# A two-block layer on one core: the second block's stores, and the transfers of its sums, issued from GpSimd's queue instead of SyncE's

## The chip, the core and the metric

The kernel runs on one core of one Trainium2 chip. The metric is the time of one execution on the device in microseconds, as the median of three runs. Engines are named as the profile names them: PE is TensorE (PEld its loading of weights), DVE is VectorE, ACT is ScalarE, POOL is GpSimd, and SP is SyncE, which computes nothing and issues transfers. SPq is SP's queue. A transfer can be issued from SP's queue or from POOL's, and each queue issues in its order: an instruction at its head that waits holds all behind it.

## The reference, cut to what matters

Two layers follow one another on 1,024 tokens of width 1,024, in float32. The first has a gated spatial branch, a state-space branch and 16 experts with 128 tokens each; the change doesn't touch it. The second, the subject here, projects its input to queries, keys, values, gates, a recurrent branch and merge gates, mixes dilated attention of three groups of four heads, runs a linear recurrence over time, and merges:

```python
h = rms_norm_2(x, g_pre) * (1 + scale) + shift
proj = h @ w_in
q, k, v, g_att, u, g_lru, merge = jnp.split(proj, split_at, axis=-1)
y_a = (dilated_attention(q, k, v) * jax.nn.silu(g_att)) @ w_pa
u = causal_depthwise_conv(u, conv_w, conv_b)
y_b = (rg_lru(u, ...) * jax.nn.silu(g_lru)) @ w_pb
gate_a, gate_b = jnp.split(jax.nn.sigmoid(merge), 2, axis=-1)
out = (gate_a * y_a + gate_b * y_b) @ w_o
return x + gate * rms_norm_2(out, g_post)
```

## The kernel before

Float32 products are made of parts: each operand is split into a high part (ScalarE, line 224, `wh`) and the rest (VectorE, line 225, `wl`), and three matmuls of 128x128 by 128x512 replace one (`mm3`).

The second block (`block2`) starts at about 1,700 us. Its projections go in pairs of 128 output columns (`Pair`, numbered by `n`): a scheme of seven products P1 to P7 instead of eight, for the two column blocks and the two halves of the tokens. For that, the pair's weights are loaded into two buffers `wr` (of four; line 217), VectorE forms sums of them (lines 505 to 508), and parts A, B, C, D are split. Pair n+1's weights are asked for when pair n has begun; split D and split C of an earlier pair free the buffers.

What a product leaves in PSUM goes through `one` or `two` of an output object. `Spill` copies or adds it into a tile `st` of 128x512 (two buffers) and stores it to DRAM (lines 416 and 418): queries, keys and values (`qd`, `kd`, `vd`; 24 stores each), the gate of the recurrence (`sgd`, 16), the attention gate (`gad`, 8) and the merge gates (`mgd`, 32). With `step` 8 (queries and keys of group 2) the store writes 1,024 runs of 256 bytes. `Merge` does the same for `yd` (16 stores, lines 440 and 446). `Keep` leaves the recurrent input in SBUF.

Three generators run beside the projections, one step per product (`tick`). `lru` makes the recurrence of one block of 128 channels and stores the result to `hgd` (line 646). `sums` then loads these results in pairs (lines 655 and 656), forms four sums and differences on GpSimd (lines 660 to 667, 128x512 each; four quarters of four) and stores them to `hs1d` to `hs4d` (line 670), for use as operands of the last projections. `attention` works head by head: loads of v, q and k (lines 690, 694, 695), scores, softmax, values, and a store of the head's result with its sums to `od` (lines 758, 761, 763; rows of 520 bytes); then it combines the groups and stores `otd` (line 830). `sums` and `attention` use the same six buffers `m0` to `m5`; the first q and k come into those that held the third quarter of `sums`.

Before the change GpSimd's queue in this block held one scatter, a few splits and subtractions at the start, eight small memsets (line 464) and the sixteen additions of `sums`. Everything that is transferred was issued from SyncE. The order of every queue is made when the kernel is built, by a scheduler that goes by the order of the program and by its own estimates of when an operand or a buffer will be ready. In the experts' part, three loads of weights are issued from GpSimd (line 1918).

Of the kernel before, what the change touches and what calls it, by code (L numbers as in the profile page):

```python
# [364 lines left out]
def block2(k, out, dbg=None):  # L365
    nc, i, c = k.nc, k.i, k.c
    V, S, SY, GP = nc.vector, nc.scalar, nc.sync, nc.gpsimd
# [3 lines left out]
    halves = [slice(0, 512), slice(512, 1024)]  # L371
# [18 lines left out]
    class Spill:  # L390
# [11 lines left out]
        def one(s, h, p):  # L402
            st, (o, p) = s.of(p)
            S.activation(o, p, AF.Copy)
            s.put(h, st)

        def two(s, h, a, b):
            st, (o, a, b) = s.of(a, b)
            V.tensor_tensor(o, a, b, op=ADD)  # L409
            s.put(h, st)  # L410

        def put(s, h, st):
            if s.step == 8:

                d = s.dst.rearrange("p (r h i) -> p h r i", r=8, h=2)
                SY.dma_start(d[:, h], st.rearrange("p (r i) -> p r i", r=8))
            else:
                SY.dma_start(s.dst[:, halves[h]], st)

    class Keep:  # L420
        def __init__(s, dst):
# [8 lines left out]
    class Merge:  # L430
# [6 lines left out]
        def one(s, h, p):  # L437
            st = k.t([128, 512], "st", 2)
            V.tensor_tensor(st, p, s.gate[:, halves[h]], op=MUL)
            SY.dma_start(s.dst[:, halves[h]], st)  # L440

        def two(s, h, a, b):
            st = k.t([128, 512], "st", 2)
            V.tensor_tensor(st, a, b, op=ADD)  # L444
            V.tensor_tensor(st, st, s.gate[:, halves[h]], op=MUL)  # L445
            SY.dma_start(s.dst[:, halves[h]], st)

    hgd = [dram(f"hgd{f}") for f in range(8)]
    hsd = {n: [dram(f"h{n}d{x}") for x in range(2)] for n in ("s1", "s2", "s3", "s4")}
# [42 lines left out]
    class Pair:  # L492
# [9 lines left out]
        def sums(s, eng=V):  # L502
            s.t = k.t([128, 1024], "t12")
            (a0, a1), (b0, b1), (t0, t1) = ((z[:, :512], z[:, 512:]) for z in (*s.raw, s.t))
            eng.tensor_tensor(t0, b0, a0, op=SUB)
            eng.tensor_tensor(t1, b1, t0, op=SUB)
            eng.tensor_tensor(b0, b1, b0, op=SUB)
            eng.tensor_tensor(a1, a1, t1, op=SUB)
# [81 lines left out]
    def lru(f, u):  # L590
        fs = slice(f, f + 1)
        uc, r = k.m(1, 1152), k.m(2, 1152)
        SY.dma_start(uc[:, 1024:], i["wrg"][:, f * 128:(f + 1) * 128])
        SY.dma_start(r[:, 1024:], i["wig"][:, f * 128:(f + 1) * 128])
        ws = [tuple(k.t([128, 128], n + q, 1, FR) for q in "hl") for n in ("wrg", "wig")]
        for raw, w in zip((uc, r), ws):
            k.split(raw[:, 1024:], *w)
        uc, r = uc[:, :1024], r[:, :1024]
        cw = cq("cw")[:, 4 * f:4 * f + 4]
        S.activation(uc, u[:, 3:], AF.Identity, scale=cw[:, 0:1], bias=cq("cb")[:, fs])  # L600
        for j in (1, 2, 3):
            V.scalar_tensor_tensor(uc, u[:, 3 - j:1027 - j], cw[:, j:j + 1], uc, op0=MUL, op1=ADD)
            yield
        if "uc" in dbg:
            SY.dma_start(dbg["uc"][f * 128:(f + 1) * 128, :], uc)
        yield
        uh, ul = k.split(uc, k.m(4, 1024, FR), k.m(3, 1024, FR))
        yield
        P = []
        for wh, wl in ws:  # L610
            for hs in halves:
                P.append(k.ps("pb"))
                k.mm3(P[-1], wh, wl, uh[:, hs], ul[:, hs], True, True)
            if not P[2:]:
                yield
        ig, d = k.m(3), k.m(4)
        for p, (b, o, hs) in zip(P, ((b, o, hs) for b, o in (("brg", r), ("big", ig)) for hs in halves)):
            S.activation(o[:, hs], p, AF.Sigmoid, bias=cq(b)[:, fs])
        yield
        V.tensor_tensor(uc, ig, uc, op=MUL)  # L620
        t = ig
        S.activation(t, r, AF.Tanh, scale=p4[:, fs])
        S.activation(r, r, AF.Exp, scale=m8[:, fs])
        yield

        S.activation(r, r, AF.Copy, scale=0.5, bias=0.5)
        V.scalar_tensor_tensor(d, t, 1.0, r, op0=ADD, op1=MUL)
        yield
        V.scalar_tensor_tensor(r, d, -2.0, r, op0=ADD, op1=MUL)
        S.activation(t, t, AF.Sqrt)  # L630
        yield
        V.tensor_scalar(d, r, -2.0, -1.0, op0=MUL, op1=ADD)
        yield
        V.scalar_tensor_tensor(r, r, -2.0, t, op0=MUL, op1=MUL)
        sg = k.m(3)
        SY.dma_start(sg, sgd[f])
        yield
        S.activation(sg, sg, AF.Silu)
        V.tensor_tensor(uc, uc, r, op=MUL)
        yield  # L640
        V.tensor_tensor_scan(out=r, data0=d, data1=uc, initial=0.0, op0=MUL, op1=ADD)
        if "lru" in dbg:
            SY.dma_start(dbg["lru"][f * 128:(f + 1) * 128, :], r)
        yield
        V.tensor_tensor(r, r, sg, op=MUL)
        SY.dma_start(hgd[f], r)

    def sums():

        lo, hi = halves  # L650
        todo = None
        for x in range(5):
            if x < 4:
                g, r, t = (k.m(3 * (x % 2) + y) for y in range(3))
                SY.dma_start(g, hgd[x])
                SY.dma_start(r, hgd[x + 4])
                yield
            if todo:
                put, g_, r_, t_ = todo
                GP.tensor_tensor(t_[:, lo], g_[:, hi], r_[:, hi], op=ADD)  # L660
                put("s1", t_[:, lo])
                GP.tensor_tensor(g_[:, hi], g_[:, lo], g_[:, hi], op=SUB)
                put("s3", g_[:, hi])
                yield
                GP.tensor_tensor(t_[:, hi], t_[:, lo], g_[:, lo], op=SUB)
                put("s2", t_[:, hi])
                GP.tensor_tensor(r_[:, lo], r_[:, lo], t_[:, hi], op=SUB)
                put("s4", r_[:, lo])
                yield
            todo = (lambda n, z, x=x: SY.dma_start(hsd[n][x // 2][:, halves[x % 2]], z)), g, r, t  # L670


    toks = [[(128 * m, 1) for m in range(8)],
# [7 lines left out]
    otd = [dram(f"otd{j}") for j in range(4)]  # L681
    tok = lambda g, m: slice(toks[g][m][0], toks[g][m][0] + 127 * toks[g][m][1] + 1, toks[g][m][1])

    class Head:
# [53 lines left out]
        def values(s, u):  # L738
            ms, W = tiles[s.g][u]
            g, n = s.g, len(ms)  # L740
            if u == 0:
                s.R = k.m(5, 1040).rearrange("p (m d) -> p m d", m=8)
            p = k.ps("pb")
            vv = lambda m: s.v[:, m * 128:(m + 1) * 128]
            for x, m in enumerate(ms):
                o = p[:, x * 128:(x + 1) * 128]
                if W == 256:
                    k.mm(o, s.pt[:, 2 * x * 128:2 * x * 128 + 128], vv(m - back[g]), True, False)
                    k.mm(o, s.pt[:, 2 * x * 128 + 128:2 * x * 128 + 256], vv(m), False, True)
                else:  # L750
                    k.mm(o, s.pt[:, x * 128:(x + 1) * 128], vv(m), True, True)
            S.activation(s.R[:, ms[0]:ms[0] + n, :128], p[:, :n * 128].rearrange("p (m d) -> p m d", m=n), AF.Copy)
            if u + 1 < len(tiles[g]):
                return
            V.tensor_copy(s.R[:, :, 128:], s.ss)
            dst = od[g, s.j]
            if g == 0:
                SY.dma_start(dst.rearrange("(m p) d -> p m d", p=128), s.R)
            elif g == 1:
                for b in range(2):  # L760
                    SY.dma_start(dst[512 * b:512 * b + 512].rearrange("(p m) d -> p m d", m=4), s.R[:, 4 * b:4 * b + 4, :])
            else:
                SY.dma_start(dst.rearrange("(p m) d -> p m d", m=8), s.R)

    def attention():
        heads = [Head(g, j) for j in range(4) for g in (0, 1)] + [Head(2, j) for j in range(4)]
# [5 lines left out]
        for x in range(len(units) + 1):  # L772
            n, u = units[x] if x < len(units) else (None, None)
            b = units[x - 1] if x else None
# [21 lines left out]
        for j in range(4):  # L796
            R = nxt
# [27 lines left out]
            for h, hs in enumerate(halves):  # L825
                p = k.ps("pb")
                for m in range(4):
                    k.tr(p[:, m * 128:(m + 1) * 128], o3[0][:, 4 * h + m, :], ident)
                S.activation(R[1][:, :1024].rearrange("p (t m) -> p m t", m=8)[:, 4 * h:4 * h + 4], p.rearrange("p (m t) -> p m t", m=4), AF.Copy)
            SY.dma_start(otd[j], R[1][:, :1024])  # L830

# [46 lines left out]
    def squares(half, t4, v):  # L880
        z = (a2 if half else F)[t4][:, :1024]
        return z, S.activation(z, xs[4 * half + t4], AF.Square, accum_out=v[:, t4:t4 + 1])
# [22 lines left out]
    for t4 in range(4):  # L905
        for h, hs in enumerate(halves):
            p = k.ps()
# [3 lines left out]
        z, sqd = squares(0, t4, va)  # L911
# [12 lines left out]
    for kk in range(8):  # L924
        dst = (a11 + a12)[kk]
# [35 lines left out]
    for kk in range(4):  # L961
        x = split("s4", kk, a12[kk])
# [120 lines left out]
    for tt in range(8):  # L1083
# [6 lines left out]
        for h, hs in enumerate(halves):  # L1090
            p = k.ps(("pa", "pb")[h])
# [3 lines left out]
            f = fb[:, hs]  # L1095
# [5 lines left out]
        r = k.rsqrt(v, 1, "or")  # L1101
# [1021 lines left out]
```

## Time and profile before

| what | value |
|---|---|
| median of three runs | 2803.3 us (2800.92 to 2807.61) |
| the profiled execution | 2800.66 us |
| its span | 2798.9 us |
| TensorE busy | 2712.4 us, 97% of the span |
| VectorE, ScalarE, GpSimd busy | 2233.9, 1653.2 and 112.6 us |
| granted clock of TensorE, mean | 0.988 |
| transfers issued by hardware queues, by GpSimd's | 655.76 MB and 20.06 MB |

Engines' busy time leaves out the issue of transfers. Matmuls are pipelined and their ends modelled, so a stretch is better judged by how many matmuls it holds than by its busy share. "DMA share" is the mean busy share of the core's 16 DMA engines. A row of a timeline has the start, the duration (or, for several, the stretch from the first start to the last end), the engine, the line, the operation, output and input, and in brackets the idle time before it with what ended it.

### The profile page before, as it was taken

What the parts mean: (1) busy time and instruction counts of PE and PEld (TensorE: products, weight loads), DVE (VectorE), ACT (ScalarE), POOL (GpSimd) and SP (SyncE); (2) the same over time, 40 slices, a digit from 0 to 9 for tenths busy, and PEclk for the clock granted to TensorE, in tenths of its full rate; (3) what the DMA queues carried; (4) which work ended last, traced back from release to release, by engine and by line L of the source; (5) the groups of instructions that cost most, each with busy time, mean ns of one, the idle gap of its engine ahead of it and who ended that gap; (6) DMA issues with size and microseconds to landing.
All of it is one profiled execution on the core that took longest, in us unless ns stands there. A gap on an engine that the chain in (4) does not pass through costs nothing. (4 is left out here: it accounts for less than half of the span.)

```text
span 2798.9 us, 37301 instructions
## 1 busy us (share of the span) xinstructions
PE 2712.4 (97%) x13379; PEld 2261.6 (81%) x13379; DVE 2233.9 (80%) x3608; ACT 1653.2 (59%) x2202; POOL 112.6 (4%) x101
## 2 busy tenths in 40 slices
PE   9999999969999999999999996999999999999998
PEld 9889887858888888888888885788888788887777
DVE  8856467579999999999999998878888555578774
ACT  6343234248888888888888886465664344445441
POOL 0000000000000000000000002000002000000000
PEclk9999999979999999999999998999999999999999
DMA  7223365568999999999999992233335654467762
GB/s 264 72 74 97 132 213 173 205 248 331 392 379 381 383 384 383 385 385 385 383 386 384 383 376 86 79 114 128 120 116 187 197 155 151 161 212 259 248 216 83
DMA packets 181995, 678.20 MB, mean 242 GB/s; under 512 B 34993, under 2 KB 46513, under 8 KB 141105
## 3 DMA queue, kind: packets, MB, share of 16 engines
q1 hardware_dynamic: 176768, 655.76, 63.6%
q0 software_dynamic: 5040, 20.06, 2.7%
q8 instruction: 105, 1.72, 0.2%
q14 instruction: 82, 0.66, 0.1%
HBM read 588.02 MB, written 85.62 MB: 241 GB/s over the span
## 5 line engine op out<-in xcount | busy, mean ns | idle before, releaser
L230 PE MATMUL ps<-A,wh 128*128 128x512 f32 x1920 | 601.8, 394 | 3.3 <-DVE u L548 1.9
L230 PEld LDWEIGHTS ps<-A,wh 128*128 128x128 f32 x1920 | 357.0, 188 | 79.2 <-DVE m L428 2.6
L230 PE MATMUL ps<-A,wl 128*128 128x512 f32 x960 | 375.0, 391 | 0.0
L1932 DVE TENSOR_TENSOR wl<-A,wh 128x1024 fp32r<-128x1024 f32 x256 | 313.3, 1224 | 50.0 <-ACT wh L1928 37.8
L1932 DVE TENSOR_TENSOR ml<-A,mh 128x1024 fp32r<-128x1024 f32 x256 | 313.0, 1223 | 17.6 <-ACT mh L1928 0.2
L230 PE MATMUL ps<-S,wh 128*128 128x512 f32 x960 | 302.5, 396 | 11.2 <-DVE u L553 9.6
L1928 ACT ACTIVATE wh<-A 128x1024 fp32r<-128x1024 f32 x256 | 271.7, 1061 | 60.3 <-PE ps L230 47.9
L1928 ACT ACTIVATE mh<-A 128x1024 fp32r<-128x1024 f32 x256 | 271.7, 1061 | 60.0 <-PE ps L230 60.0
L224 ACT ACTIVATE wh<-wr 128x512 fp32r<-128x512 f32 (+2 forms) x168 | 154.1, 919 | 213.6 <-PE ps L230 160.2
L230 PEld LDWEIGHTS ps<-S,wh 128*128 128x128 f32 x960 | 178.9, 189 | 50.4 <-DVE u L553 12.1
L225 DVE TENSOR_TENSOR wl<-wr,wh 128x1024 fp32r<-128x1024 f32 (+2 forms) x166 | 175.9, 1060 | 51.7 <-ACT wh L224 37.0
L230 PEld LDWEIGHTS ps<-A,wl 128*128 128x128 f32 x960 | 180.2, 188 | 38.7 <-issue 0.7
L230 PE MATMUL ps<-mh,xh 128*128 128x512 f32 x520 | 206.3, 397 | 0.0
L230 PE MATMUL ps<-wh,xh 128*128 128x512 f32 x520 | 203.1, 391 | 0.0
L230 PE MATMUL ps<-wh,xl 128*128 128x512 f32 x520 | 203.0, 390 | 0.0
L230 PE MATMUL ps<-wl,xh 128*128 128x512 f32 x520 | 202.7, 390 | 0.0
L230 PE MATMUL ps<-ml,xh 128*128 128x512 f32 x520 | 202.5, 389 | 0.0
L230 PE MATMUL ps<-mh,xl 128*128 128x512 f32 x520 | 202.5, 389 | 0.0
L230 PE MATMUL ps<-S,wl 128*128 128x512 f32 x480 | 188.2, 392 | 0.4 <-DVE wl L225 0.4
L230 PE MATMUL ps<-wh,A 128*128 128x256 f32 (+1 forms) x708 | 142.5, 297 | 5.2 <-ACT A L1132 5.2
L230 PEld LDWEIGHTS ps<-wh,A 128*128 128x128 f32 x708 | 114.8, 195 | 8.8 <-ACT A L1132 5.2
L409 DVE TENSOR_TENSOR st<-u,ps 128x512 f32<-128x512 f32 x96 | 76.9, 801 | 53.4 <-PE ps L230 50.5
(525 smaller groups left out, 5474.6 us busy)
## 6 DMA issues: line engine op xcount, KB each, us to landing
A<-in_w_up_dram SPq DMA_DIRECT2D x125, 1024.0 KB, 8.2
A<-in_w_gate_dram SPq DMA_DIRECT2D x64, 1024.0 KB, 8.7
A<-in_w_down_dram SPq DMA_DIRECT2D x64, 1024.0 KB, 7.7
wr<-in_w_gate_dram SPq DMA_DIRECT2D x124, 512.0 KB, 7.6
mr<-in_w_down_dram SPq DMA_DIRECT2D x59, 1024.0 KB, 7.6
wr<-in_w_in_dram SPq DMA_DIRECT2D x81, 512.0 KB, 3.9
wr<-in_w_mod_dram SPq DMA_DIRECT2D x24, 512.0 KB, 4.6
wr<-in_w_ing_dram SPq DMA_DIRECT2D x16, 512.0 KB, 4.2
```

The source lines that it names most:

```text
L224: s.parts = (s.nc.scalar.activation(hi, raw, AF.Copy), (eng or s.nc.vector).tensor_tensor(lo, raw, hi, op=OP.subtract))
L225: (eng or s.nc.vector).tensor_tensor(lo, raw, hi, op=OP.subtract))
L230: s._pe(out, s.nc.tensor.matmul(out, a, b, start=start, stop=stop, skip_group_check=True))
L409: V.tensor_tensor(o, a, b, op=ADD)
L1928: k.hi = a = S.activation(h, raw, AF.Copy)
L1932: x = V.tensor_tensor(l, raw, h, op=OP.subtract)
```

## The change

The engine that issues 196 transfers is changed from SyncE (`SY`) to GpSimd (`GP`): the stores of `Spill` and `Merge`, the store of `hgd`, loads and stores of `sums`, the stores of `od` and of `otd`. The loads of weights, of the attention's operands and of gates stay on SyncE.

```diff
             if s.step == 8:
 
                 d = s.dst.rearrange("p (r h i) -> p h r i", r=8, h=2)
-                SY.dma_start(d[:, h], st.rearrange("p (r i) -> p r i", r=8))
+                GP.dma_start(d[:, h], st.rearrange("p (r i) -> p r i", r=8))
             else:
-                SY.dma_start(s.dst[:, halves[h]], st)
+                GP.dma_start(s.dst[:, halves[h]], st)
...
             V.tensor_tensor(st, p, s.gate[:, halves[h]], op=MUL)
-            SY.dma_start(s.dst[:, halves[h]], st)
+            GP.dma_start(s.dst[:, halves[h]], st)
...
             V.tensor_tensor(st, st, s.gate[:, halves[h]], op=MUL)
-            SY.dma_start(s.dst[:, halves[h]], st)
+            GP.dma_start(s.dst[:, halves[h]], st)
...
         V.tensor_tensor(r, r, sg, op=MUL)
-        SY.dma_start(hgd[f], r)
+        GP.dma_start(hgd[f], r)
...
-                SY.dma_start(g, hgd[x])
-                SY.dma_start(r, hgd[x + 4])
+                GP.dma_start(g, hgd[x])
+                GP.dma_start(r, hgd[x + 4])
...
-            todo = (lambda n, z, x=x: SY.dma_start(hsd[n][x // 2][:, halves[x % 2]], z)), g, r, t
+            todo = (lambda n, z, x=x: GP.dma_start(hsd[n][x // 2][:, halves[x % 2]], z)), g, r, t
...
             if g == 0:
-                SY.dma_start(dst.rearrange("(m p) d -> p m d", p=128), s.R)
+                GP.dma_start(dst.rearrange("(m p) d -> p m d", p=128), s.R)
             elif g == 1:
                 for b in range(2):
-                    SY.dma_start(dst[512 * b:512 * b + 512].rearrange("(p m) d -> p m d", m=4), s.R[:, 4 * b:4 * b + 4, :])
+                    GP.dma_start(dst[512 * b:512 * b + 512].rearrange("(p m) d -> p m d", m=4), s.R[:, 4 * b:4 * b + 4, :])
             else:
-                SY.dma_start(dst.rearrange("(p m) d -> p m d", m=8), s.R)
+                GP.dma_start(dst.rearrange("(p m) d -> p m d", m=8), s.R)
...
-            SY.dma_start(otd[j], R[1][:, :1024])
+            GP.dma_start(otd[j], R[1][:, :1024])
```

## Rows read from the trace of the kernel before

**Rows 1.** The page's first part: busy us, share of the span, instructions.

```profile
PE 2712.4 (97%) x13379; PEld 2261.6 (81%) x13379; DVE 2233.9 (80%) x3608; ACT 1653.2 (59%) x2202; POOL 112.6 (4%) x101
```

**Rows 2.** Busy time by stretches: length, busy and count by engine, clock, DMA share, GB/s.

```profile
1860.00:1960.00 100.00, 99.57 (x439) 82.00 (x438) 83.97 (x98) 58.51 (x69) 0.30 (x3) 1.00 0.33 117
...
2160.00:2170.00 10.00, 10.00 (x45) 8.26 (x44) 5.81 (x6) 2.72 (x3) 8.26 (x6) 1.00 0.97 317
2170.00:2190.00 20.00, 15.64 (x62) 12.44 (x61) 9.49 (x11) 4.30 (x5) 5.25 (x4) 0.91 0.86 283
...
2570.00:2580.00 10.00, 8.61 (x38) 6.79 (x38) 10.00 (x12) 6.42 (x7) 0.00 (x0) 1.00 0.90 307
2620.00:2660.00 40.00, 37.32 (x163) 29.93 (x162) 27.10 (x35) 18.25 (x20) 0.00 (x0) 1.00 0.72 242
```

**Rows 3.** TensorE's waits in the second block: us in total, times, longest.

```profile
PE ps L230 <- DMA m<-kd: 1.9, 1, 1.9
```

**Rows 4.** Timeline of all engines, 2164 to 2200 us.

```profile
2177.64 1.06 ACT L224 ACTIVATE wh<-wr 128x1024 fp32r<-128x1024 f32 x1 [4.88 <-DMA wr<-in_w_in_dram]
...
2181.57 0.88 PE L230 MATMUL ps<-S,wh 128*128 128x512 f32 x2 [4.36 <-DVE u L553]
...
2191.92 0.38 PE L230 MATMUL ps<-m,m 128*128 128x128 f32 x2
```

**Rows 5.** Timeline of VectorE, splits that free a weight buffer, 2098 to 2165 us.

```profile
2126.65 1.22 DVE L225 TENSOR_TENSOR wl<-wr,wh 128x1024 fp32r<-128x1024 f32 x1
...
2147.18 1.21 DVE L225 TENSOR_TENSOR wl<-wr,wh 128x1024 fp32r<-128x1024 f32 x1
...
2153.24 1.39 DVE L225 TENSOR_TENSOR wl<-wr,wh 128x512 fp32r<-128x512 f32 x1 [2.33 <-ACT wh L224]
```

**Rows 6.** Timeline of SyncE's queue, 2100 to 2340 us.

```profile
2118.50 8.58 SPq L418 DMA_DIRECT2D qd<-st  x3
2127.89 0.33 SPq L217 DMA_DIRECT2D wr<-in_w_in_dram  x1
...
2169.01 1.90 SPq L217 DMA_DIRECT2D wr<-in_w_in_dram  x2
...
2184.41 0.56 SPq L416 DMA_DIRECT2D qd<-st  x1
2185.02 0.66 SPq L694 DMA_DIRECT2D m<-qd  x1
```

**Rows 7.** Timeline of all engines in the experts' part, 600 to 625 us.

```profile
604.63 1.22 DVE L1932 TENSOR_TENSOR wl<-A,wh 128x1024 fp32r<-128x1024 f32 x1
605.36 0.61 POOL L1918 DMA_DIRECT2D A<-in_w_down_dram  x1 [0.78 <-DVE ml L1932]
```

**Rows 8.** Transfers by issuer, 580 to 680 us: count, KB each, median us to landing.

```profile
A<-in_w_down_dram POOLq DMA_DIRECT2D x2, 1024.0 KB, 7.2
A<-in_w_down_dram SPq DMA_DIRECT2D x2, 1024.0 KB, 4.8
```

**Rows 9.** Transfers by issuer in the second block, 1650 to 2799 us.

```profile
vd<-st SPq DMA_DIRECT2D x24, 256.0 KB, 2.0
...
m<-kd SPq DMA_DIRECT2D x12, 512.0 KB, 5.0
...
hs3d<-m SPq DMA_DIRECT2D x4, 256.0 KB, 5.6
```

**Rows 10.** The page's costliest groups: busy us, mean ns, idle before.

```profile
L409 DVE TENSOR_TENSOR st<-u,ps 128x512 f32<-128x512 f32 x96 | 76.9, 801 | 53.4 <-PE ps L230 50.5
```

**Rows 11.** Timeline of GpSimd in the second block.

```profile
2150.07 1.39 POOL L660 TENSOR_TENSOR m<-m,m 128x512 f32<-128x512 f32 x1 [119.72 <-DMA kd<-st]
...
2172.71 1.43 POOL L660 TENSOR_TENSOR m<-m,m 128x512 f32<-128x512 f32 x1 [3.02 <-DMA hs1d<-m]
...
2176.85 1.27 POOL L667 TENSOR_TENSOR m<-m,m 128x512 f32<-128x512 f32 x1
```

**Rows 12.** Waits of all engines, 2610 to 2660 us.

```profile
DVE st L444 <- DMA yd<-st: 5.8, 2, 4.1
```

## The prediction

> **What bounds the kernel.** I read the page's first part, then the busy time by stretches, then the waits and the order of time in the stretches that fall short. TensorE is busy for 97% of the span [rows 1], so only its holes can be won. In the projections of the second block there are none: 439 matmuls in 100 us, one each 0.228 us [rows 2]. The reader is to see three stretches below that pace: 2170 to 2190 with 62 matmuls where 87.8 fit, 2570 to 2580 with 38 for 43.9, 2620 to 2660 with 163 for 175.6 [rows 2], and one short wait for a load of keys [rows 3]. At 0.228 us the three are worth 5.9, 1.3 and 2.9 us, the wait 1.9: 12.0 us is all that better queues can give.
>
> The first has a plain cause. ScalarE waits 4.88 us for a piece of `w_in`, and TensorE then 4.36 us for what VectorE makes behind it [rows 4]; the granted clock over the 20 us is 0.91 [rows 2], below the 2.4 GHz level, so part of it ran at 1.2 GHz. An earlier load of weights left the moment a split freed its buffer: split over at 2126.65 + 1.22 = 2127.87, load at 2127.89 [rows 5, 6]. The next two such splits end at 2148.40 and 2154.63 [rows 5], but the next loads leave from 2169.01 on [rows 6], 21 and 14 us late. No buffer held them: SyncE's queue was working through the sums of the recurrent branch and the projections' stores.
>
> **What moves.** 196 transfers leave SyncE for GpSimd: 128 stores of projections, 16 of `yd`, 8 of `hgd`; in `sums` 8 loads and 16 stores; 16 stores of `od` and 4 of `otd`. None is added, and bytes and arithmetic stay.
>
> Issue. SyncE needs 0.33 us for one [rows 6], GpSimd took 0.61 for a plain 1 MB load [rows 7]. 196 x 0.61 = 120 us, on a queue that has little else from 1763 to 2662: its idleness covers them. No row shows a store from GpSimd, nor one in 1,024 short runs, of which there are 20 (16 of `qd` and `kd` with `step` 8, 4 of `od` for g = 0). Such an issue lies between 0.6 and 8 x 0.61 = 4.9 us, since the load with a price has 128 rows; I take 1 to 2, nearer to the row.
>
> Landing. In one stretch a 1 MB load took 7.2 us from GpSimd and 4.8 from SyncE [rows 8], so a move costs up to 2.4 us; a gain isn't excluded where loads stand ahead of the store on SyncE's queue. A store lands in 2.0 us in the median [rows 9], from GpSimd then in 2.0 to 4.4. The buffer `st` has two places. The first and the third store of a pair leave 8.58 - 0.33 = 8.25 us apart [rows 6] and an eviction takes 0.80 [rows 10], so the third eviction begins 7.4 us after the first one's end; 0.6 + 4.4 = 5.0 us is in time: cost 0. With 4.9 us of issue it is 9.3, 1.9 late, in four pairs. VectorE is busy for 9.49 of the 20 us in which those pairs begin [rows 2], and TensorE has four banks ahead. I take 0.5 us for all short runs, ends 0 and 7.6.
>
> Descriptors. GpSimd issued that load in 0.61 us from 605.36 on, while a VectorE subtraction ran from 604.63 to 605.85 [rows 7]: it wasn't held until the subtraction's end and a full issue more. The Trainium skill (SBUF — State Buffer, Who interferes with whom) says that VectorE in a two-port mode shuts GpSimd out of a shared port pair for a whole instruction, and starves the descriptors of a GpSimd DMA. By that rule a store could wait for one VectorE instruction more; at 1.22 us that makes 6.2 against 7.4, nothing on the path, and only with short runs would it add to the third rival.
>
> Weights. With stores and sums gone, the loads leave at about 2148.4 and 2154.6. The late one took 2177.64 - 2169.01 = 8.6 us [rows 4, 6]; so both have landed by 2163.2, ahead of 2172.8, when ScalarE began to wait. Term: -5.9 us, ends 0 (the 16 DMA engines are 0.97 busy from 2160 on [rows 2] and may pass nothing sooner) and -5.9.
>
> What is late next. TensorE then reaches the first scores of attention at 2191.92 - 5.9 = 2186.0 [rows 4]. Their loads of q and k left from 2185.02 on, behind a store of `qd` that had waited for VectorE [rows 6]; that holder goes. But their buffers come from the third quarter of `sums`, which now shares one queue with its own transfers. Before, its sixteen additions ran from 2150.07 to 2178.12 [rows 11]. After, a quarter is four additions of 1.3 and four issues of 0.61 us, 7.6; four quarters and four issues of loads make 32.9 us, end 2183.0. If both later pairs of loads stand at the queue's head until the stores of the quarter before have landed (5.6 us [rows 9]; the additions had a wait of 3.02 there [rows 11]), it is 11.2 us more. The third quarter's last addition ends 7.6 us sooner, its store takes 0.6 + 5.6 and the load 5.0 [rows 9]: q and k are there between 2186.6 and 2197.8, that is 0.6 to 11.8 us late. A hole costs more than its wait, as 5.9 for 4.36 did (1.35 times): 0.6 to 16 us. I take 2, near the lower end, because the builder orders every queue by its own estimate of readiness and places the scores later when it sees the sums end later. The projections' stores behind those loads wait as they did on SyncE.
>
> The other holes. The 1.9 us for `kd` [rows 3]: its loads no longer stand behind stores, but their buffer is freed late too; 1 us, ends 0 and 1.9. At 2570 VectorE is busy for all 10 us [rows 2]; only the lateness of loads behind a store can go: 0.5, ends 0 and 1.3. In 2620 to 2660 VectorE waits 5.8 us for `st` to be stored to `yd` [rows 12]; these stores now have a queue without loads, but the rest of that hole is waits for loads of `gad`, which stay: 1.5, ends 0 and 2.9.
>
> **Sum.** -5.9 + 2 + 0.5 - 1 - 0.5 - 1.5 = -6.4 us. The profiled execution took 2800.7 us (span 2798.9 and 1.8 around it): 2794.3. The median shown is 2.6 us above it: 2796.9 us, 0.23% below 2803.3.
>
> **Rivals.**
> *No change, 2800 to 2804 us.* The weights leave sooner but land no sooner, or the hole moves on to the scores: 5.9 won, about 6 lost, and the small gains remain. For it: the share of 0.97 [rows 2]. Against: that share is read from 2160 on, and the loads leave at 2148 and 2155. The Trainium skill (DMA: Bandwidth & Descriptors, Issuing engines are not separate DMA queues) says that all queues run on the same engines and a second issuer saves only issue time; the full engines agree with it, but the loads that left 21 and 14 us late are a wait that it doesn't speak of.
>
> *Slower by the sums, up to 2810.9 us.* One mechanism: the loads of `sums` stand on GpSimd's queue until its own stores have landed, additions and stores behind them, and q and k behind those. At the full 11.8 us the term of 2 becomes 16: 2796.9 + 14. It decides, by more than 0.2%, from about 10.6 us of waiting on (10.6 x 1.35 = 14.3, less the 2 taken and the 6.4 won: 5.9). For it: two rounds of 5.6 us. Against: before, the wait of the additions for a store was 3.02 us [rows 11], not 5.6.
>
> *Slower by short runs, 2806 to 2816 us.* Issue 4.9 and landing 7.2 us [rows 8] make 12.1 against 7.4: 4.7 us in each of four pairs, 19 of VectorE, half of it hidden or none. It decides from some 12 us of passed-on waits. Against: VectorE is half idle there.
>
> *All holes close.* 12.0 us: 2788.7 for the profiled execution, 2791.3 as a median.
>
> **Chances.** Forecast 0.41, all holes 0.05, no change 0.31, sums 0.14, short runs 0.09. Within 0.2% (5.6 us) is about what a measurement of this kernel can't tell from no change. Faster 0.46, same 0.31, slower 0.23. Leaving out the outer part of the short runs, the range is 2790 to 2811; the likeliest case's own is 2791 to 2799.
>
> **What would show it.** Right: the two loads issued near 2148 and 2155, no wait of ScalarE on them, the clock full from 2170 to 2190, issues on GpSimd near 0.6 us, third evictions that wait for no store. Wrong: TensorE waiting for q, k or v after the last addition; issues of several microseconds for `qd`, `kd` or `od`; VectorE waiting for `st`; or an order of queues that opens holes before 2140, where TensorE has none now.

## The result, and the profile after

The changed kernel took 2826.5 us (median of 6), the kernel before beside it 2801.75: 1.0085 times as long, 95% interval 1.0074 to 1.0096, some 24 us slower. The forecast was 2796.9 us, range 2790 to 2811. One of the six runs took 3423.39 us and is left out of the ratio.

The first part of the page and its two largest queues, after (packets, MB, share of 16 engines):

```profile
PE 2719.4 (96%) x13379; PEld 2265.8 (80%) x13379; DVE 2240.2 (79%) x3608; ACT 1653.5 (59%) x2202; POOL 223.2 (8%) x297
q1 hardware_dynamic: 130624, 596.93, 57.1%
q0 software_dynamic: 22512, 78.89, 8.5%
```

Beside [rows 1] the arithmetic is the same. GpSimd's busy time grew by 110.6 us: unlike what stands beside the profile of before, issues do count as busy on this engine, and the 196 took 0.56 us each. TensorE's busy time grew by only 7 us, so most of the 24 is idle. To see where, one row per stage is enough. Line 505, on VectorE, runs once in each pair, so the same pair can be found in both traces. Three of its 38 rows, before and then after: ahead of the sums, in the attention, and the last pair's:

```profile
2148.31 0.68 DVE L505 TENSOR_TENSOR t<-wr,wr 128x512 f32<-128x512 f32 x1
2295.97 0.68 DVE L505 TENSOR_TENSOR t<-wr,wr 128x512 f32<-128x512 f32 x1
2617.53 0.69 DVE L505 TENSOR_TENSOR t<-wr,wr 128x512 f32<-128x512 f32 x1
```

```profile
2149.81 0.70 DVE L505 TENSOR_TENSOR t<-wr,wr 128x512 f32<-128x512 f32 x1
2301.13 0.68 DVE L505 TENSOR_TENSOR t<-wr,wr 128x512 f32<-128x512 f32 x1
2634.76 0.69 DVE L505 TENSOR_TENSOR t<-wr,wr 128x512 f32<-128x512 f32 x1
```

The lag is 1.5 us up to the sums, 5.2 once the attention runs, 17.2 at the last pair and 25.7 at the end (spans 2824.6 and 2798.9). So three stretches lose: +3.7, +12.1 and +8.5 us. The projections before them lose nothing.

**First stretch.** The foreseen part came. Issues on SyncE's queue, ScalarE's split, and windows (columns as in [rows 2]), after:

```profile
2149.94 0.33 SPq L217 DMA_DIRECT2D wr<-in_w_in_dram  x1
```

```profile
2176.61 1.06 ACT L224 ACTIVATE wh<-wr 128x1024 fp32r<-128x1024 f32 x1 [1.55 <-PE ps L230]
```

```profile
2160.00:2170.00 10.00, 9.40 (x42) 7.51 (x41) 7.55 (x6) 2.72 (x3) 6.32 (x8) 1.00 0.76 250
2170.00:2190.00 20.00, 17.70 (x78) 14.29 (x77) 10.65 (x9) 4.90 (x6) 18.01 (x22) 1.00 0.82 286
2190.00:2200.00 10.00, 3.83 (x10) 3.18 (x11) 6.96 (x10) 0.17 (x1) 5.38 (x7) 0.53 0.81 236
```

The load leaves 19 us earlier than the late one of [rows 6], ScalarE waits for TensorE instead of for weights [rows 4], and 2170 to 2190 holds 78 matmuls instead of 62 [rows 2]. But 2190 to 2200 holds 10, at a granted clock of 0.53, about the 1.2 GHz level, behind the wait that [rows 3] had at 1.9 us. Waits, GpSimd's queue, two evictions (ScalarE's, then VectorE's) and TensorE, after:

```profile
DVE st L409 <- DMA qd<-st: 10.9, 1, 10.9
PE ps L230 <- DMA m<-kd: 9.5, 3, 8.5
```

```profile
2151.50 1.50 POOL L660 TENSOR_TENSOR m<-m,m 128x512 f32<-128x512 f32 x1 [0.83 <-DMA hgd<-m]
...
2186.44 1.30 POOL L662 TENSOR_TENSOR m<-m 128x512 f32<-128x512 f32 x1
2187.66 0.92 POOL L416 DMA_DIRECT2D qd<-st  x1
2188.45 0.67 POOL L670 DMA_DIRECT2D hs3d<-m  x1
...
2191.60 1.49 POOL L667 TENSOR_TENSOR m<-m,m 128x512 f32<-128x512 f32 x1
```

```profile
2174.47 0.58 ACT L404 ACTIVATE st<-ps 128x512 f32<-128x512 f32 x1
...
2192.67 1.07 DVE L409 TENSOR_TENSOR st<-u,ps 128x512 f32<-128x512 f32 x1 [10.90 <-DMA qd<-st]
```

```profile
2196.17 0.77 PE L230 MATMUL ps<-m,m 128*128 128x128 f32 x2 [8.47 <-DMA m<-kd]
```

The last of the sixteen additions ends at 2193.1 us instead of 2178.1 [rows 11]. From the first addition (2151.5) to the last, GpSimd's queue also holds 25 issues, 14.6 us together, and two loads of `sums` stand at its head for 3.6 and 1.6 us, mostly until a store of `hs4d` has landed. So the store of a tile that ScalarE had filled by 2175.1 us was issued at 2187.7, and the eviction that needs the tile again waits 10.9 us for its landing. TensorE waits 8.5 us for keys: their load left at 2191.3, when a store of the third quarter had landed from the buffer that it goes into.

Line 505 shows the gain and the loss apart. Two pairs after the one at 2148 the lag is -2.2 us, with the weights' gain; at the next pair it is 6.7, and 5.2 from the pair at 2269 on.

**Second stretch.** The head of SyncE's queue, and two waits behind it, 2480 to 2650 us, before and after:

```profile
SPq L793 <- DMA otd<-m: 1.1, 1, 1.1
SPq L980 <- DMA otd<-m: 0.8, 1, 0.8
DVE cmn L803 <- DMA m<-od: 5.5, 3, 3.2
PE ps L230 <- DVE u L553: 3.8, 4, 1.4
```

```profile
SPq L980 <- DMA otd<-m: 8.3, 2, 7.7
SPq L793 <- DMA otd<-m: 7.3, 2, 5.5
DVE cmn L803 <- DMA m<-od: 11.0, 3, 6.9
PE ps L230 <- DVE u L553: 11.2, 4, 4.6
```

A load of the next heads' `od` (L793), and later one of `hgd` (L980), goes into the buffer from which `otd` was stored, and stands at the queue's head until that store has landed. The loads come late, the combination (L803) waits for them, VectorE falls behind, TensorE waits. Landings from each queue in the second block, after and then before:

```profile
vd<-st POOLq DMA_DIRECT2D x24, 256.0 KB, 2.3
yd<-st POOLq DMA_DIRECT2D x16, 256.0 KB, 4.9
otd<-m POOLq DMA_DIRECT2D x4, 512.0 KB, 5.6
```

```profile
yd<-st SPq DMA_DIRECT2D x16, 256.0 KB, 3.8
otd<-m SPq DMA_DIRECT2D x4, 512.0 KB, 2.9
```

**Third stretch.** The last store of `yd` and ScalarE's first split into a buffer `B`, before and after:

```profile
2661.91 0.32 SPq L446 DMA_DIRECT2D yd<-st  x1
...
2666.11 1.06 ACT L224 ACTIVATE B<-wr 128x1024 fp32r<-128x1024 f32 x1 [1.38 <-DVE wl L225]
```

```profile
2679.77 0.54 POOL L446 DMA_DIRECT2D yd<-st  x1 [5.09 <-DVE st L445]
...
2685.72 1.06 ACT L224 ACTIVATE B<-wr 128x1024 fp32r<-128x1024 f32 x1 [5.59 <-DMA yd<-st]
```

`B` belongs to a pool (a region of on-chip memory) that opens where that of the projections closes, so its first use needs the last store out of the old one to have landed. Before, the split began 4.2 us behind that store's issue and had waited for VectorE, not for the store. After, it begins 5.95 us behind it and waits for the store: ScalarE's queue stands for 5.6 us, the next splits of `w_pa` behind it. Near the end TensorE waits longer for a `B` of ScalarE, before and after:

```profile
PE ps L230 <- ACT B L224: 2.3, 1, 2.3
```

```profile
PE ps L230 <- ACT B L224: 7.0, 1, 7.0
```

After, 2720 to 2740 holds 46 matmuls where the same stage before, 2700 to 2720, held 77:

```profile
2720.00:2740.00 20.00, 13.02 (x46) 10.07 (x46) 14.19 (x15) 5.76 (x7) 0.00 (x0) 0.83 0.45 156
```

```profile
2700.00:2720.00 20.00, 17.66 (x77) 14.14 (x77) 15.69 (x23) 6.45 (x9) 0.00 (x0) 1.00 0.34 105
```

### The profile page after: what moved, and what is told of

Read it like the earlier page. It is cut to its first block, busy times and chain, and to the rows that moved or that the text cites. A ratio compares the mean times of both kernels' runs of the same rounds, so it can differ in the third digit from the quotient of the medians.

```text
span 2824.6 us, 37354 instructions
## 1 busy us (share of the span) xinstructions
PE 2719.4 (96%) x13379; PEld 2265.8 (80%) x13379; DVE 2240.2 (79%) x3608; ACT 1653.5 (59%) x2202; POOL 223.2 (8%) x297
## 4 chain that ended last, share of the span: by engine, by line
PE 78%; issue 9%; DVE 6%; DMA 3%; ACT 2%; POOL 2%; SPq 0%; POOLq 0%; DVEq 0%; ACTq 0%
PE ps L230 76%; PE ps L233 3%; DVE m L1643 1%; DMA m<-kd 1%; DMA hs4d<-m 1%; DVE wl L225 0%; POOL mgd L418 0%; DMA m<-mgd 0%; ACT wh L224 0%; ACT U L1273 0%; DVE m L1853 0%; DVE S L871 0%; DVE m L885 0%; DMA wr<-in_xT_dram 0%; DMA wr<-in_xp_dram 0%
```

## The experiments

The theory: three separate delays, each from transfers that somebody waits for soon. The rivals: one delay that the rest inherits; or a general cost of GpSimd's stores or of the other order of the queues. "Attention", "heads" and "end" are the three stretches as lags of the profiled execution against before, from L505 as above. A trace also holds lag from before the sums (up to 5.7 us in e15, 2.2 in e7, whose edit lies after them); it is left out. Each kernel has one trace, and kernels with the same work in a stretch differ in it by some 3 us in the first two and by up to 6 in the last (e5 and e6). So the timing decides; the stretches tell where. Microseconds beside a ratio are its share of the time before; they can differ by up to 3 us from the difference between the two medians.

| kernel | ratio to before, interval | attention | heads | end |
|---|---|---|---|---|
| changed | 1.0085 (1.0074 to 1.0096) | +3.7 | +12.1 | +8.5 |
| e1 changed, sums on SyncE | 1.0074 (1.0056 to 1.0091) | +0.9 | +10.8 | +4.6 |
| e2 changed, od and otd on SyncE | 1.0052 (1.0033 to 1.0071) | +1.6 | +1.1 | +5.5 |
| e3 changed, yd on SyncE | 1.0073 (1.0055 to 1.0090) | +3.7 | +12.8 | +1.8 |
| e4 Spill alone | 1.0010 (1.0000 to 1.0020) | +0.4 | +0.8 | +1.8 |
| e6 od alone | 0.9997 (0.9987 to 1.0007) | -2.0 | +0.7 | +4.0 |
| e7 otd alone | 1.0021 (1.0011 to 1.0031) | -2.8 | +3.8 | -0.7 |
| e8 yd alone | 1.0026 (1.0017 to 1.0036) | -0.7 | +1.1 | +7.2 |
| e12 sums alone | 1.0025 (1.0016 to 1.0035) | +9.3 | -1.8 | +3.4 |
| e14 sums' stores alone | 1.0016 (1.0007 to 1.0026) | +7.0 | -1.4 | -0.6 |
| e11 yd but its last pair | 1.0008 (0.9998 to 1.0018) | -2.1 | -1.0 | +3.8 |
| e9 additions on VectorE, alone | 0.9989 (0.9979 to 1.0000) | -3.3 | -1.8 | +1.1 |
| e5 Spill, additions on VectorE | 0.9986 (0.9977 to 0.9996) | -6.5 | +1.0 | -1.8 |
| e15 sums, additions on VectorE | 0.9994 (0.9984 to 1.0004) | -2.8 | -2.4 | +2.4 |
| e10 changed, additions on VectorE | 1.0047 (1.0032 to 1.0062) | -2.8 | +9.9 | +6.6 |
| e13 e10, otd and last yd on SyncE | 1.0008 (0.9999 to 1.0018) | -3.4 | +2.6 | +4.4 |
| e16 Spill, od, most of yd, additions | 1.0001 (0.9991 to 1.0010) | -8.2 | +2.9 | -0.5 |

### One part taken back (e1 to e3)

e1, against the changed kernel (lines 646, 655, 656, 670):

```diff
-        GP.dma_start(hgd[f], r)
+        SY.dma_start(hgd[f], r)
...
-                GP.dma_start(g, hgd[x])
-                GP.dma_start(r, hgd[x + 4])
+                SY.dma_start(g, hgd[x])
+                SY.dma_start(r, hgd[x + 4])
...
-            todo = (lambda n, z, x=x: GP.dma_start(hsd[n][x // 2][:, halves[x % 2]], z)), g, r, t
+            todo = (lambda n, z, x=x: SY.dma_start(hsd[n][x // 2][:, halves[x % 2]], z)), g, r, t
```

> The changed kernel with the store of hgd and the loads and stores of sums back on SyncE; Spill, Merge, od and otd stay on GpSimd. Theory (three separate delays, each from transfers that something waits for soon): the third quarter's additions no longer stand behind their own loads' waits, the wait of TensorE for kd at the start of attention falls from 9.5 us to under 3, and the time falls by 5 to 10 us against the changed kernel, to 2816 to 2821; the losses from 2500 on stay. Rival A (one delay at the start of attention that all the rest inherits): the whole 24 us come back, 2800 to 2804. Rival B (the 128 stores of projections, which land later from GpSimd everywhere, or the planner's other order): no change, 2824 to 2829.

2821.3 us. TensorE's wait for `kd` is gone, but VectorE still waits, 9.6 us for a store of `vd`. Rival A, by which all 24 us would come back, falls. The gain itself, 3 us, is not shown by the timing: the interval of 1.0074 holds the changed kernel's 1.0085.

e2, against the changed kernel (the stores of lines 758, 761 and 763 alike, and 830):

```diff
-                GP.dma_start(dst.rearrange("(m p) d -> p m d", p=128), s.R)
+                SY.dma_start(dst.rearrange("(m p) d -> p m d", p=128), s.R)
...
-            GP.dma_start(otd[j], R[1][:, :1024])
+            SY.dma_start(otd[j], R[1][:, :1024])
```

> The changed kernel with the stores of od and otd back on SyncE. Theory: the wait of VectorE's cmn for od (longest 6.9 us) and of SyncE's load of hgd for otd (7.7 us) fall to 4 or less, the losses between 2500 and 2640 (from +5 to about +17 us of lag) mostly go, and the time falls by 7 to 12 us, to 2814 to 2820. Rival A (one inherited delay from the start of attention): no more than 2 us, 2824 to 2829. Rival B (projection stores, planner's order): the same, 2824 to 2829.

2814.2 us, 9 us less than the changed kernel by the ratios: 11 of the 12 us of the second stretch go, the wait of L803 falls to 1.3, that of L980 to 2.9. Rival B falls for this stretch.

e3, against the changed kernel (lines 440 and 446 alike):

```diff
-            GP.dma_start(s.dst[:, halves[h]], st)
+            SY.dma_start(s.dst[:, halves[h]], st)
```

> The changed kernel with the stores of yd back on SyncE. Theory: the last stores of yd free the space into which the first split of w_o writes; from SyncE they land 1 us sooner and are issued sooner, the wait of ScalarE for yd (5.6 us) and of TensorE behind it (7.0 us) go, and the time falls by 6 to 9 us, to 2817 to 2821. Rival (the last stores of yd are late because the tail of the projections is late, wherever they are issued): 0 to 2 us, 2824 to 2829, and the wait of ScalarE stays above 4 us.

2821.7 us; ScalarE's wait for `yd` falls to 1.7 and the last stretch from 8.5 to 1.8, the other two stay. Its ratio gives back 3.4 us, half of what the trace does, and its interval holds 1.0085; what `yd` costs is therefore read from e8 and e11.

### One part alone (e4, e6 to e8, e11, e12, e14)

e4, against the kernel before (lines 416 and 418):

```diff
-                SY.dma_start(d[:, h], st.rearrange("p (r i) -> p r i", r=8))
+                GP.dma_start(d[:, h], st.rearrange("p (r i) -> p r i", r=8))
...
-                SY.dma_start(s.dst[:, halves[h]], st)
+                GP.dma_start(s.dst[:, halves[h]], st)
```

> The kernel before with the 128 stores of Spill alone on GpSimd; sums, hgd, yd, od and otd stay on SyncE. Theory: projections' stores have time, so nothing is lost, and part of the weights' wait at 2172 (5.9 us) may go, since SyncE's queue loses the stores that stood ahead of those loads: 2796 to 2803 against 2801.75 before. Rival B (the projections' stores or the planner's order carry the loss): 2815 to 2829.

1.0010: two thirds of the transfers cost some 2.8 us, at the edge of their interval, and win nothing. Why nothing is won, from the timelines of GpSimd, and of ScalarE and VectorE:

```profile
2166.39 1.30 POOL L667 TENSOR_TENSOR m<-m,m 128x512 f32<-128x512 f32 x1
2167.63 1.09 POOL L418 DMA_DIRECT2D vd<-st  x2
```

```profile
2157.20 0.58 ACT L404 ACTIVATE st<-ps 128x512 f32<-128x512 f32 x1
...
2174.08 0.69 DVE L409 TENSOR_TENSOR st<-u,ps 128x512 f32<-128x512 f32 x1 [9.58 <-DMA vd<-st]
```

Both stores stand behind eight additions (2155.4 to 2167.7), though ScalarE had filled the first tile by 2157.8 us and VectorE the second by 2164.5. VectorE waits 9.6 us for the first to land, and TensorE 5.7 behind it.

e6 and e7 are the two edits of e2 the other way round, each alone, from the kernel before:

```diff
-                SY.dma_start(dst.rearrange("(m p) d -> p m d", p=128), s.R)
+                GP.dma_start(dst.rearrange("(m p) d -> p m d", p=128), s.R)
```

```diff
-            SY.dma_start(otd[j], R[1][:, :1024])
+            GP.dma_start(otd[j], R[1][:, :1024])
```

> The kernel before with the 16 stores of od alone on GpSimd. Both stores of the heads together (od and otd) carried about 11 us between 2490 and 2640 us of the changed kernel's 24. Theory: of these od carries the smaller part, by the wait of VectorE's cmn for a load of od at 2510 to 2540 (6.9 us against 3.2): 2 to 5 us slower than before, 2802 to 2806 against 2800. Rival: od starts the whole chain (cmn late, otd late, the loads of hgd late), and carries all of it: 8 to 12 us slower. Second rival: nothing, within 2 us, as the lateness came from the sums before it.

> The kernel before with the 4 stores of otd alone on GpSimd. Theory: otd landed 5.6 us after its issue from GpSimd and 2.9 from SyncE, and loads of hgd into the same buffers stand at the head of SyncE's queue until it has (7.7 us): 4 to 8 us slower than before, 2804 to 2808. Rival: the otd stores are late only because od before them is; then within 2 us of before.

`od`: no difference, though it lands in 6.5 us instead of 5.1 (e6's own landings). `otd`: 1.0021, 5.9 us (4.3 between the medians), with four transfers; SyncE's queue shows the two waits of the changed kernel:

```profile
SPq L793 <- DMA otd<-m: 7.5, 2, 5.7
SPq L980 <- DMA otd<-m: 4.8, 2, 4.6
```

e8 and e11, from the kernel before; e11 chooses the queue by the pair:

```diff
-            SY.dma_start(s.dst[:, halves[h]], st)
+            GP.dma_start(s.dst[:, halves[h]], st)
```

```diff
-            s.dst, s.gate = yd[m], k.m(q)
+            s.dst, s.gate = yd[m], k.m(q); s.by = GP if m < 6 else SY
...
-            SY.dma_start(s.dst[:, halves[h]], st)
+            s.by.dma_start(s.dst[:, halves[h]], st)
```

> The kernel before with the 16 stores of yd alone on GpSimd. Theory: the last of them land later and the first split of w_o into the space they free waits for them, as in the changed kernel (5.6 us of ScalarE, 7.0 us of TensorE behind it): 4 to 7 us slower than before, 2804 to 2807, all of it after 2640 us. Rival: on a queue with nothing else the stores leave as soon as they are ready, and the wait needs the other delays as well: within 2 us of before, and no such wait.

> The kernel before with the stores of yd on GpSimd, except those of the last pair (m = 6 and 7), which stay on SyncE: 12 of 16 move. Theory (only the last store of yd has someone waiting for it, ScalarE's first split of w_o into the space that it frees): the 5 to 7 us that yd alone cost are gone, within 2 us of before, and ScalarE waits less than 2 us for yd. Rival (all stores of yd land later and hold VectorE's tile st through the last pairs): still 4 to 7 us slower.

e8: 1.0026, 7.3 us (4.6 between the medians), on a queue that holds nothing else in that stretch; ScalarE waits 5.6 us for `yd`. With the last pair's four stores back on SyncE that wait is 1.4 and the ratio 1.0008. So by the ratios about two thirds of it are the last pair's stores. ScalarE's waits in e8 and in e11:

```profile
ACT B L224 <- DMA yd<-st: 5.6, 1, 5.6
```

```profile
ACT B L224 <- DMA yd<-st: 1.4, 1, 1.4
```

In e11's last stretch 3.8 us remain without the long wait, as in e6 and e12 (4.0 and 3.4), which move no `yd` at all; that much is within what single traces differ by.

e12 and e14, from the kernel before: e12 is the edit of e1 the other way round, e14 (shown) the same without the loads:

```diff
-        SY.dma_start(hgd[f], r)
+        GP.dma_start(hgd[f], r)
...
-            todo = (lambda n, z, x=x: SY.dma_start(hsd[n][x // 2][:, halves[x % 2]], z)), g, r, t
+            todo = (lambda n, z, x=x: GP.dma_start(hsd[n][x // 2][:, halves[x % 2]], z)), g, r, t
```

> The kernel before with the stores of hgd and the loads and stores of sums alone on GpSimd; Spill, yd, od and otd stay on SyncE. The other parts alone gave +2.8 (Spill), -0.8 (od), +5.9 (otd) and +7.3 us (yd), 15.2 together of the 24. Theory 1 (parts add up): 6 to 10 us slower, with a wait of TensorE for kd at the start of attention above 4 us. Theory 2 (the sums hurt only together with Spill, whose stores stand behind them on the same queue): within 3 us of before, and SyncE's loads of weights leave earlier than 2165 us, where they left at 2169 before.

> The kernel before with the stores of hgd and of sums alone on GpSimd; the loads of sums stay on SyncE. All of them on GpSimd cost 7.1 us. Theory A (the loads wait at the head of GpSimd's queue for its own stores to land, and hold additions behind them): most of the 7.1 goes, -1 to +3 us against before, and the sixteenth addition ends before 2186 us (2192.0 with all of them on GpSimd, 2178.1 before). Theory B (sixteen issues of 0.55 us between sixteen additions, and stores that land later): 5 to 8 us slower, and the sixteenth addition ends after 2187 us.

Parts add up, as far as five intervals of 0.001 to either side can tell: 1.0010, 0.9997, 1.0021, 1.0026 and 1.0025 make 0.0079 of 0.0085. e12's loads of weights leave at 2150.0 and 2155.8, as forecast for the change, and it is 7 us slower all the same. With the loads of the sums taken off the queue (e14) the last addition ends at 2191.2, e12's at 2192.0; less the lag that each trace had at 2148 (4.3 and 1.6) that is 8.7 and 12.3 us later than in [rows 11]. So the loads at the queue's head account for some 3.5 of 12.3. The times, 1.0016 and 1.0025, agree with that, but their intervals overlap. The larger part is additions and issues in one line, and what they wait for:

```profile
2156.92 1.29 POOL L660 TENSOR_TENSOR m<-m,m 128x512 f32<-128x512 f32 x1 [6.23 <-DMA hgd<-m]
2158.50 0.56 POOL L670 DMA_DIRECT2D hs1d<-m  x1 [0.30 <-POOL m L660]
...
2189.89 1.29 POOL L667 TENSOR_TENSOR m<-m,m 128x512 f32<-128x512 f32 x1
```

(e14: first addition, its store, last addition. The first also comes 6.8 us later than in [rows 11], 2.5 more than that lag; it waits for the store of `hgd`, now on GpSimd too.)

### The additions off GpSimd's queue (e5, e9, e10, e15)

All four move the sixteen additions (lines 660 to 667): e9 in the kernel before, e5 in e4, e15 in e12, e10 in the changed kernel.

```diff
-                GP.tensor_tensor(t_[:, lo], g_[:, hi], r_[:, hi], op=ADD)
+                V.tensor_tensor(t_[:, lo], g_[:, hi], r_[:, hi], op=ADD)
...
-                GP.tensor_tensor(r_[:, lo], r_[:, lo], t_[:, hi], op=SUB)
+                V.tensor_tensor(r_[:, lo], r_[:, lo], t_[:, hi], op=SUB)
```

> The kernel before with the 128 stores of Spill on GpSimd and, beside that, the sixteen additions of sums on VectorE, so that GpSimd's queue holds no additions ahead of stores. Theory: with Spill alone on GpSimd the store of vd stood behind the additions there, VectorE's eviction waited 9.6 us for it and TensorE 5.7 us behind that, and the gain for the weights was lost; here that wait of VectorE for vd falls below 3 us, the additions take less than 1 us each instead of 1.3, the first scores of attention come earlier, and the time is 4 to 8 us below that of Spill alone: 2795 to 2800, or 0 to 5 us below before. Rival: the loss is the later landing of stores from GpSimd and not their place in its queue; then VectorE still waits over 6 us for vd or qd, and the time stays at 2803 to 2807; with VectorE's 11 us of additions more on top it may be worse.

> The kernel before with the sixteen additions of sums on VectorE and every transfer on SyncE as before. The run with Spill on GpSimd and the additions on VectorE was 4 us faster than before. Theory 1 (it needs both: SyncE free of stores so that weights leave early, and GpSimd's queue free of additions): here the wait of ScalarE for a piece of w_in near 2177 us (4.9 us before) stays above 2, and the time is within 3 us of before, 2799 to 2805. Theory 2 (the additions alone: the sums end earlier, so the attention starts earlier, whoever issues the stores): 4 to 7 us faster, 2795 to 2798.

> The changed kernel with the sixteen additions of sums on VectorE; all 196 transfers stay on GpSimd. Theory (at the start of attention the additions and the loads' waits on GpSimd's queue hold the stores of vd and qd, and VectorE waits for these): the waits of VectorE for qd (10.9 us) and of TensorE for kd (9.5 us) fall below 4, and the time falls by 5 to 10 us to 2816 to 2821; the rest, from otd and yd after 2500 us, stays. Rival (the loads of sums at the head of the queue hold it all the same): the waits stay above 6 us and the time falls by less than 3.

> The kernel before with the stores of hgd and the loads and stores of sums on GpSimd and the sixteen additions on VectorE. Theory A (loads that wait for landings): VectorE's additions still stand behind those loads' landing, 3 to 7 us slower than before. Theory B (additions and issues share one queue): the additions leave it, within 2 us of before or faster, to 2797.

e5 is faster than before, 2797.1 us against 2802.5. Its last addition, first scores and windows:

```profile
2173.23 0.68 DVE L667 TENSOR_TENSOR m<-m,m 128x512 f32<-128x512 f32 x1
```

```profile
2186.05 0.38 PE L230 MATMUL ps<-m,m 128*128 128x128 f32 x2
```

```profile
2170.00:2190.00 20.00, 20.00 (x95) 16.66 (x94) 14.09 (x20) 6.30 (x7) 3.09 (x4) 1.00 0.80 290
```

The scores start at 2186.05 us, where the prediction had wanted them (2186.0), and 2170 to 2190 has no hole. e9 lies between its theories: 2799.0 us, 0.9989, the wait for weights down from 4.9 to 2.5 us. That speaks for the additions' time being on the path already before the change, though the interval reaches 1. In the traces e5 gains 6.5 us at the attention's start and e9 3.3; the timings don't separate them. e10 takes 11 us off the changed kernel, with TensorE's wait for `kd` down to 0.4 and VectorE's for `qd` to 4.6. e15 against e12 (0.9994 and 1.0025) speaks for theory B.

These runs hold two changes in one, since an addition is also shorter on VectorE (0.69 us against 1.3). e9 gives the price of that where no store is on GpSimd: 0.0011. Against their partners the others win more: e5 0.0024, e15 0.0031, e10 0.0038. The rest, 0.0013 to 0.0027 or some 4 to 8 us, is put down to the queue; for e5 alone it is within the noise.

### The three places together (e13, e16)

e13 is e10 with `otd` (e2's last line) and the last pair of `yd` (e11's lines) on SyncE: 188 of 196 transfers stay on GpSimd. e16 is e5 with `od` (e6) and `yd` but for the last pair (e11) on GpSimd as well:

```diff
-            GP.dma_start(otd[j], R[1][:, :1024])
+            SY.dma_start(otd[j], R[1][:, :1024])
```

> The changed kernel with three edits: the sixteen additions of sums on VectorE, the 4 stores of otd on SyncE, the 4 stores of the last pair of yd on SyncE; 188 of 196 transfers stay on GpSimd. Theory (these three places carry the loss): from 2815.7 with the additions alone moved, less 5.9 for otd and 7.3 for yd: 2799 to 2806 beside 2802 before. Rival (the landing of the many other stores carries a part of its own, between 2500 and 2640 us, as od did together with otd): 2808 or more.

> The additions of sums on VectorE, and on GpSimd the stores of Spill (128), of od (16) and of yd but for the last pair (12), 156 transfers; sums, otd and the last pair of yd on SyncE. Theory (these parts cost nothing alone, and the additions on VectorE let the weights' gain through): 2795 to 2800, 3 to 7 us faster than before, as Spill and the additions alone (2797.1 against 2802.5). Rival (they add up to more late landings between 2500 and 2660 us): 2802 to 2808.

e13: 2806.1 us, the upper edge of what was expected, 1.0008; three edits take back 22 of 24 us. From e10 to e13, which puts only the four stores of `otd` and the last four of `yd` back, it is 11 us (9 between what each has over its median before). What the additions on VectorE win by themselves (0.9989) it does not show; 0.0019, some 5 us, thus lie with the other stores, and how stays open. e16 shows no gain: 1.0001. Its trace is 5.8 us ahead of before, counted from the pair at 2148, but that execution was the fastest of its ten, 6 us below their median. The rival isn't excluded. The fastest remains e5.

## Why the prediction was wrong

Two steps failed. The cost of 0 for landings asked only when `st` comes free, and left out the next users of the buffers of `otd` and of the last `yd`. And the 2 us for the scores, with the line that GpSimd's idleness covers the issues, left out what issues do between additions.

**Weights, -5.9.** Right in the mechanism. The loads left at 2149.9 and 2157.0, no wait of ScalarE on them, the clock full from 2170 to 2190, and TensorE ready for the scores at 2187.7 us instead of 2191.9. The Trainium skill (DMA: Bandwidth & Descriptors, Issuing engines are not separate DMA queues) says that a second issuer saves only the time of issuing. In e12 the loads left at 2150.0 and 2155.8 us instead of 2169.0: what stood ahead of them in the queue held them, and of that the rule doesn't speak. But the gain had no exit, as next.

**Scores late, +2 of 0.6 to 16.** The step that failed first. The bounds held: the additions were given an end between 2183.0 and 2194.2, and it was 2193.1. The low end counted 20 issues and no wait; there were 25, six of them stores of projections, and 5.3 us of standing, and the third quarter's last addition ended at 2184.1 us instead of 2175.4. The choice near the lower end rested on the builder putting the scores later, and it did not: TensorE stood 8.5 us. The sentence that the projections' stores "wait as they did on SyncE" was wrong too, since SyncE has no additions in its line. Weights, scores, short runs and the wait for `kd` were to make -4.4 together; they made +3.7.

**Landing, cost 0.** Medians of 2.3 to 2.6 us for `vd`, `kd` and `qd` from GpSimd are within 2.0 to 4.4 (the store that VectorE waited for took 4.9), and e4 shows that 128 such stores cost little. But the working asked only whether the tile `st` comes free in time. For `otd` and the last `yd`, the next user of the buffer is a load at the head of SyncE's queue and a split at the head of ScalarE's; nothing in the sum priced either, and the eight stores cost some 11 us (e10 and e13). Nor was the third eviction free where additions stood ahead: it waited up to 10.9 us. (The 8.25 us taken between the first and the third store of a pair lie between the second and the fourth; the other two are 9.2 apart, and nothing hangs on it.) **The other holes, -0.5 and -1.5,** stand where +12.1 and +8.5 were measured: 22.6 of the 30.6 us between the forecast and the traces.

**Short runs, +0.5.** Issues of 0.84 to 1.01 us against 1 to 2 taken and 4.9 as bound; that rival is out. **Descriptors.** The 112 plain stores of line 418 were issued in 0.54 to 0.62 us each beside a VectorE that was 79% busy: no issue was held for an instruction of VectorE.

**The rival by the sums** named the right place, but loads that wait for landings, its mechanism, are the smaller part in e12 and e14, and its price of 14 us was not reached: the sums alone cost 7 (e12). *No change* fits e4 alone: the weights' gain moved on to a wait for a store.

## What to carry to other kernels

Before a store is moved to another queue, ask who takes over its buffer, and on which queue that user stands at the head: here 4 stores of `otd` and the last 4 of `yd` cost some 11 us (e7, with e8 less e11; e10 less e13), 128 projection stores 3. A queue of an engine that computes is only idle between its computations: behind sixteen additions and their transfers stores came so late that VectorE waited for up to 10.9 us. A gain at one wait counts only if the next thing on the path is early too; read when its operands come before booking it.

## What the runs showed of the hardware

A plain store is issued by GpSimd in 0.54 us (0.32 by SyncE), one of 1,024 runs of 256 bytes in 0.84 to 1.01. By the medians `vd` (256 KB) landed in 2.3 us from GpSimd and 2.0 from SyncE, `yd` (256 KB) in 4.9 and 3.8, `otd` (512 KB) in 5.6 and 2.9, and in 6.3 where `otd` was the only one moved (e7). An addition of 128x512 took 1.3 us on GpSimd and 0.69 on VectorE. After a wait of 8.5 us TensorE's granted clock was 0.50 from 2196 to 2200 us, the 1.2 GHz level, and a 128x512 matmul took 0.63 us there instead of 0.39; from 2202 on the clock was full again. So the wait cost more than it lasted.
